# Short products of a two-block transformer kernel laid over all 128 rows of the array, beside zeros

## The chip, the core and the metric

The kernel runs on one core of a Trainium2 chip. A core has a matrix engine (TensorE, in the profile PE, with its weight loads as PEld), VectorE (DVE), ScalarE (ACT), GpSimd (POOL) and SyncE (SP), which here issues the DMAs. Each engine works through its own queue in order; between engines stand semaphores. The metric is the device time of one execution in microseconds (us); the median of the runs counts, and less is better.

## What is computed

Two blocks, one after the other, on 512 tokens of width 1024 in float32. The first block has one layer: a mixer with a state space part (8 heads of 64, two groups with a state of 64) and a stick-breaking attention (8 heads of 64), a cross attention to 256 memory positions, and a feed-forward with squared relu. The second block puts 16 learned tokens ahead (528 positions) and has two layers: gated linear attention over chunks of 64 tokens (4 heads, keys of 128, values of 256), and a sparse attention that scores all keys with 8 small heads of 64, keeps up to 128 of them per query and attends to these; each is followed by a gated feed-forward. The parts that the change is about, from the reference:

```python
logits = jnp.einsum("bhqd,bhkd->bhqk", qb, kb) * scale        # stick-breaking: d = 64
...
S = jnp.exp(tot[:, :, 0, :, None]) * S + jnp.einsum(
    'bhcd,bhce->bhde', ki.astype(jnp.float32) * jnp.exp(tot - cum), vi.astype(jnp.float32))   # c = 64 (first: 16)
...
s_idx = jnp.einsum('bqhd,bsd->bqhs', qib, k_idx) * IDX_DIM ** -0.5    # d = 64
```

In each of them the sum runs over 64 terms, or 16 for the learned tokens.

## The kernel before

All operands of the matrix engine are pairs: a float32 number is split into a high part, in a rounded format that the engine takes at full rate, and a low part, the rest. A product is three matmuls, high by high, high by low and low by high (`mm3`; `mm` is the one place, line 231, where matmuls are issued, and `tr`, line 248, the one for transposes, so nearly all TensorE rows of the profile name one of these two lines). The split is a copy on ScalarE (`hi`, line 272) and a subtraction on VectorE or GpSimd (`lo`, line 275, the engine given by `lo_eng`).

Most of the work are dense products with weight tiles of 128 x 128, in one fixed order (`_tiles`). The weights come in units of 8 tiles by DMA and are split in half units of 4, at most two half units ahead (`w_adv`, three buffers). `dense` runs over the 8 parts of the width, three matmuls each, for 512 token columns, or for 272 and 256 of them in the second block (`FR`). The results lie in PSUM: four banks for dense products (`ps_d`, tag pd) and four for all else (`ps_s`, tag pss).

All else, the side work, is written as generators. `Sched` runs them between the steps of the dense products: each matmul adds its planned time to a clock (`sc.now`), a generator yields how long to wait in this planned time, and `tick` runs those that are due. The build then fixes the order of each engine's queue from a model of the times.

The sites that the change touches:

- `bcast` (418) and `narrow_nat` (521): transposes that bring a norm's column, or a narrow product, from one layout to the other. For the 16 learned tokens and for narrow products they use 16 or 64 rows.
- `mixer` (541): `pair` computes the queries and keys of two heads as one tile of 128 rows, head 0 in rows 0 to 63, head 1 in rows 64 to 127; `ev_q` scales and splits it into two slots of the ring "m" (16 slots). The ring later takes the memory's keys and values and the attention's output. Pairs 0 to 2 are computed beside the state space part, pair 3 behind the values, when `sb_attn` (996) has begun.
- `sb_attn`: for each head and block of 128 queries, `s1` multiplies 64 rows of queries by 64 rows of keys (tile names m,m), then come sigmoids, a running product on VectorE, transposes and the product with the values.
- `ssd` (829): the same with B and C, two groups of 64 rows; `xd` is a tile of its own.
- `gla` (1174): `transp` brings keys and values to a layout by token, 4 blocks of 128, that is two chunks of 64 rows in each (knh, knl, vnh, vnl), and 16 rows for the learned tokens (km, vm). `head` goes through the chunks: products of 64 rows, then the state (`S`, split into Sh and Sl), which the queries' product reads. Then a norm with its own tiles. The gates' narrow product has 48 rows.
- `dsa` (1590): `scores` multiplies queries by the index keys (kih, kil), which lie twice, one above the other, over 128 rows; the second matmul takes only 64 of them. `select` finds the highest scores by 16 rounds of a maximum and a replacement on VectorE. `vproj`, `s2` and `pv` treat the 16 learned tokens as products of 16 rows (vm, pTm).

Of the kernel before, what the change touches and what calls it, by code (L numbers as in the profile page):

```python
# [28 lines left out]
# heads' queries and keys, halves of their values  # L29
# [6 lines left out]
def _tiles():  # L36
# [40 lines left out]
    # second block, first layer  # L77
# [16 lines left out]
    # second layer  # L94
# [66 lines left out]
# a norm's delay behind the last of its squares, the wait before its broadcast (both in us of the tensor  # L161
# engine's work), and whether the dense products queue behind its sums (1), its broadcast (2)
# [15 lines left out]
class Sched:  # L178
    """Runs side work between the steps of the dense products, in the order of the tensor engine's time."""
# [32 lines left out]
class Kern:  # L212
# [95 lines left out]
    def w_adv(self, h):  # L308
        """splits up to half unit h + 2, loads 3 units beyond"""
# [60 lines left out]
    def norm_add(self, n, src, scale=1.0, last=False):  # L370
        """src [128, c0:c1] values by token"""
# [17 lines left out]
    def norm_fin(self, n, dim, eps, wait, urg, bc=True):  # L389
        """generator: n.col[:, i] by token of block i, n.b [128, T2] by token on every partition"""  # L390
# [27 lines left out]
    def bcast(self, out, blocks, col):  # L418
        """out[:, a + j] = col[j, i] for each block (a, m) = blocks[i]"""
# [19 lines left out]
    def after(self, n, fn, cap=2):  # L439
        """fn() once the norm is there; at most cap wait"""  # L440
# [42 lines left out]
    def start2(self):  # L483
        """constants that are needed later"""
# [56 lines left out]
    def mixer(self):  # L541
# [6 lines left out]
        def mslot():  # L548
            return self.til(mix, [P, 512], "m", 16, F32R)
# [54 lines left out]

        def pair(p):
            ((ps, _, _),) = self.dense("w_in", xs, XR)
            q = ev_q(ps, 0.125)
# [16 lines left out]
        # y * silu(z), sums of its squares  # L624
# [37 lines left out]
        # keys and values of the memory  # L662
# [101 lines left out]
    def resid(self, n, rng, norm, xs, g):  # L764
        """the n-th tile of the residual is there: parts of its product with the gain, sums of squares"""
# [63 lines left out]
    def ssd(self, pool, nm, xc, y4, tdt):  # L829
# [4 lines left out]
        BT, CT = [], []  # L834
        for src, dst, nme in ((xc[4], BT, "B"), (xc[5], CT, "C")):
            hi, lo = self.til(pool, [P, 512], nme + "h", 1, F32R), self.til(pool, [P, 512], nme + "l", 1, F32R)
            self.split(hi, lo, src)
            dst += [hi, lo]
# [1136 lines left out]
```

## Time and profile before

| what | value |
|---|---|
| time, median of 3 runs | 2020.23 us (2015.2 to 2020.8) |
| span of the profiled execution | 2017.2 us |
| its time outside the span | not listed apart; the runs lie from 2.0 us below this span to 3.6 above |
| instructions | 29258, of them 11341 matmuls and transposes |
| mean granted clock of TensorE | 0.992 |

How to read the rows that follow: a row of the timeline has start and duration in us, engine, line, operation, the tile written and those read, and the form. The form `64*128 64x256` of a matmul is the weights' rows and columns, then rows and columns of what streams through; the first number, 64, is the rows of the array that the product uses. A row of a tile's view has the count, the shortest, median and longest duration in ns, and the first and last start in us. A row of the windows has, for one stretch of the span, the busy time of each engine with its count of instructions, then the granted clock (PEclk) and the DMAs. A row of the waits has who waited for whom, the sum in us, how often and the longest. A row of the groups has the count, the busy time in us and the mean in ns, and behind a bar the idle time ahead of them. Matmuls are pipelined: a row's duration reaches from its start to the end of its last result, so durations overlap, and the pace is read from start to start.

### The profile page before, as it was taken

What the parts mean: (1) busy time and instruction counts of PE and PEld (TensorE: products, weight loads), DVE (VectorE), ACT (ScalarE), POOL (GpSimd) and SP (SyncE); (2) the same over time, 40 slices, a digit from 0 to 9 for tenths busy, and PEclk for the clock granted to TensorE, in tenths of its full rate; (3) what the DMA queues carried; (4) which work ended last, traced back from release to release, by engine and by line L of the source; (5) the groups of instructions that cost most, each with busy time, mean ns of one, the idle gap of its engine ahead of it and who ended that gap; (6) DMA issues with size and microseconds to landing.
All of it is one profiled execution on the core that took longest, in us unless ns stands there. A gap on an engine that the chain in (4) does not pass through costs nothing.

```text
span 2017.2 us, 29258 instructions
## 1 busy us (share of the span) xinstructions
PE 1986.5 (98%) x11341; PEld 1704.1 (84%) x11341; DVE 1117.3 (55%) x2040; ACT 857.5 (43%) x1636; POOL 358.1 (18%) x323
## 2 busy tenths in 40 slices
PE   8999998999999999999999999999999999999998
PEld 6877777788888888989999999998778888888886
DVE  7788876643344566666444334444898654433444
ACT  6565755542244443445433223333446543323332
POOL 2243342200000211111211001113373021101111
PEclk9999999999999999999999999999999999999999
DMA  5212221422322321212322223323221133233332
GB/s 165 73 64 63 86 71 53 151 94 94 95 94 94 95 75 53 64 43 75 100 85 94 95 84 95 95 86 95 62 74 59 35 96 94 95 94 95 97 96 79
DMA packets 53386, 171.81 MB, mean 85 GB/s; under 512 B 7224, under 2 KB 10808, under 8 KB 53248
## 3 DMA queue, kind: packets, MB, share of 16 engines
q1 hardware_dynamic: 53248, 169.95, 26.9%
q8 instruction: 89, 1.46, 0.3%
q14 instruction: 49, 0.40, 0.1%
HBM read 166.76 MB, written 4.81 MB: 85 GB/s over the span
## 4 chain that ended last, share of the span: by engine, by line
PE 94%; DVE 4%; ACT 1%; issue 1%; POOL 0%; DMA 0%; SPq 0%; DVEq 0%; POOLq 0%
PE pd L231 83%; PE pss L231 9%; PE pss L248 2%; DVE xl L284 1%; DVE swork L1703 1%; DVE m L1702 1%; DVE wlo L275 0%; POOL nacc L387 0%; DVE o L1516 0%; DMA hT<-xT 0%; DVE madd L1707 0%; ACT xh L283 0%; DVE hT L738 0%; ACT whi L272 0%; POOL hT L657 0%
## 5 line engine op out<-in xcount | busy, mean ns | idle before, releaser
L272 ACT ACTIVATE whi<-wraw 128x512 fp32r<-128x512 f32 x600 | 377.0, 630 | 818.2 <-PE pd L231 773.8
L231 PE MATMUL pd<-xh,whi 128*128 128x512 f32 (+2 forms) x2064 | 695.5, 338 | 6.3 <-ACT xh L283 5.5
L231 PE MATMUL pd<-xl,whi 128*128 128x512 f32 (+2 forms) x2064 | 696.2, 338 | 2.2 <-DVE xl L284 2.1
L231 PE MATMUL pd<-xh,wlo 128*128 128x512 f32 (+2 forms) x2064 | 695.8, 338 | 0.4 <-DVE wlo L275 0.3
L275 DVE TENSOR_TENSOR wlo<-wraw,whi 128x512 fp32r<-128x512 f32 x564 | 420.8, 748 | 425.7 <-ACT whi L272 412.0
L231 PEld LDWEIGHTS pd<-xl,whi 128*128 128x128 f32 x2064 | 390.7, 189 | 49.2 <-DVE xl L284 4.3
L231 PEld LDWEIGHTS pd<-xh,whi 128*128 128x128 f32 x2064 | 389.5, 189 | 49.0 <-ACT xh L283 5.9
L231 PEld LDWEIGHTS pd<-xh,wlo 128*128 128x128 f32 x2064 | 390.7, 189 | 45.1 <-DVE wlo L275 1.8
L231 PE MATMUL pd<-hh,whi 128*128 128x512 f32 (+2 forms) x795 | 272.4, 343 | 0.0
L231 PE MATMUL pd<-hl,whi 128*128 128x512 f32 (+2 forms) x795 | 272.0, 342 | 0.0
L231 PE MATMUL pd<-hh,wlo 128*128 128x512 f32 (+2 forms) x795 | 272.0, 342 | 0.0
L387 POOL TENSOR_TENSOR nacc<-nacc,nsq 128x512 f32<-128x512 f32 (+2 forms) x60 | 84.0, 1401 | 561.9 <-ACT nsq L385 556.3
L231 PEld LDWEIGHTS pd<-hh,wlo 128*128 128x128 f32 x795 | 149.4, 188 | 19.3
L231 PEld LDWEIGHTS pd<-hl,whi 128*128 128x128 f32 x795 | 149.4, 188 | 18.8
L231 PEld LDWEIGHTS pd<-hh,whi 128*128 128x128 f32 x795 | 149.4, 188 | 18.6
L1444 POOL TENSOR_TENSOR swg<-swg,nb 128x528 f32<-128x528 f32 (+1 forms) x44 | 57.6, 1308 | 546.5 <-ACT swg L1443 546.5
L1446 DVE TENSOR_TENSOR swg<-pd,swg 128x272 f32<-128x272 f32 (+1 forms) x66 | 32.3, 516 | 64.2 <-PE pd L231 63.6
L1442 DVE TENSOR_TENSOR swg<-pd,nb 128x272 f32<-128x272 f32 (+2 forms) x66 | 32.3, 517 | 64.1 <-PE pd L231 59.7
L275 POOL TENSOR_TENSOR wlo<-wraw,whi 128x512 fp32r<-128x512 f32 x36 | 47.3, 1317 | 61.9 <-ACT whi L272 57.3
L284 DVE SCALAR_TENSOR_TENSOR xl<-hT,cols,xh 128x512 fp32r<-128x512 f32 (+2 forms) x56 | 50.9, 920 | 13.2 <-ACT xh L283 13.0
L283 ACT ACTIVATE xh<-hT,cols 128x512 fp32r<-128x512 f32 (+2 forms) x56 | 36.9, 663 | 26.1 <-DVE hT L1463 9.5
L1086 DVE SCALAR_TENSOR_TENSOR tmp<-pd,nb 128x512 f32<-128x512 f32 x32 | 22.0, 691 | 45.8 <-PE pd L231 44.5
(490 smaller groups left out, 2533.9 us busy)
## 6 DMA issues: line engine op xcount, KB each, us to landing
wraw<-w SPq DMA_DIRECT2D x299, 512.0 KB, 3.5
rrep<-rrow SPq DMA_DIRECT2D x8, 328.0 KB, 6.9
T<-rrep SPq DMA_DIRECT2D x8, 264.0 KB, 2.5
hT<-xT SPq DMA_DIRECT2D x8, 256.0 KB, 5.4
out_dram<-o SPq DMA_DIRECT2D x8, 256.0 KB, 2.2
tmp<-memT SPq DMA_DIRECT2D x8, 128.0 KB, 2.3
wraw<-w SPq DMA_DIRECT2D x2, 256.0 KB, 3.9
qih<-tmp SPq DMA_DIRECT2D x4, 128.0 KB, 2.2
```

Of the source, the lines that this page charges most:

```text
L231: i = self.nc.tensor.matmul(out, lhsT, rhs, start=start, stop=stop)
L248: return self.nc.tensor.transpose(out, in_, self.ident[:n, :n]).ins
L272: self.nc.scalar.activation(out, in_, AF.Copy, scale=scale)
L275: (eng or self.nc.vector).tensor_sub(out, in_, hi.bitcast(F32))
L283: ins = self.nc.scalar.activation(hi, in_, AF.Copy, scale=g)
L284: self.nc.vector.scalar_tensor_tensor(lo, in_, g, hi.bitcast(F32), op0=OP.mult, op1=OP.subtract)
L387: eng.tensor_add(n.acc[:, n.c0 : n.c1], n.acc[:, n.c0 : n.c1], sq[:, n.c0 : n.c1])
L1086: nc.vector.scalar_tensor_tensor(u[:, X], ps, 0.0, nff.b[:, X], op0=OP.max, op1=OP.mult)
L1442: nc.vector.tensor_mul(g[:, c0:c1], p, nf.b[:, c0:c1])
L1444: nc.gpsimd.tensor_mul(g[:, A], g[:, A], nf.b[:, A])
L1446: nc.vector.tensor_mul(g[:, c0:c1], p, g[:, c0:c1])
L1702: nc.vector.max(m8, src)
```

## The change

Every product over 64, 48 or 16 rows gets operands of 128 rows (96 for the 48), of which those that don't belong to it are zero in one of the two.

- Queries of the stick-breaking attention: `ev_heads` makes two pairs of tiles for each pair of heads, each with one head in its half of the rows and zeros, laid by GpSimd, in the other. The keys stay as they are: the other head's rows meet zeros. The ring has 18 slots in place of 16; a pair takes 6 in place of 4.
- State space part: the same with C. To make room, `xd` becomes a temporary tile (`tmp`, three buffers in all).
- Linear attention: the keys by token get 8 blocks, one for each chunk, with zeros in the other half of the rows; two such sets are made once. The first tokens' keys get 128 rows, zeros below the 16, and their values 128 rows of whatever tokens stand there. The tile "ol" has one buffer in place of two, and the norm's two tiles become `q0` and a temporary one. The gates' 48 rows become 96.
- Scores: the second matmul takes all 128 rows; beside the product that it made, this adds the one of the two low parts.
- Sparse attention: the learned tokens' values get zeros below their 16 rows, and their probabilities 128 rows.
- Transposes in `bcast` and `narrow_nat` take 128 rows.

The number of matmuls stays. The rest of the diff takes out comments. Its core:

```diff
@@ bcast @@
-            src = col[:m, i : i + 1].to_broadcast([m, P])
+            src = col[:, i : i + 1].to_broadcast([P, P])
             if m < P:
                 pm = self.ps_s()
-                ins = self.tr(pm[:, :m], src, m)
+                ins = self.tr(pm[:, :P], src)
@@ narrow_nat @@
-        nc.scalar.copy(r[:64, :512], ps[:64, :512])
+        nc.scalar.copy(r[:, :512], ps[:, :512])
...
-            self.tr(pt[:, 64 * i : 64 * i + 64], r[:64, P * i : P * (i + 1)], 64)
-        v = pt[:, :256].rearrange("p (b c) -> p b c", b=4)
+            self.tr(pt[:, P * i : P * (i + 1)], r[:, P * i : P * (i + 1)])
+        v = pt.rearrange("p (b c) -> p b c", b=4)
@@ mixer @@
-            return self.til(mix, [P, 512], "m", 16, F32R)
+            return self.til(mix, [P, 512], "m", 18, F32R)
...
+        def ev_heads(ps, scale):
+            t = self.tmp()
+            nc.vector.scalar_tensor_tensor(t[:, :512], ps, scale, nm.b[:, X], op0=OP.mult, op1=OP.mult)
+            out = []
+            for x in range(2):
+                r, o = slice(64 * x, 64 * x + 64), slice(64 - 64 * x, 128 - 64 * x)
+                hi, lo = mslot(), mslot()
+                nc.gpsimd.memset(hi[o].bitcast(F32), 0.0)
+                nc.gpsimd.memset(lo[o].bitcast(F32), 0.0)
+                self.split(hi[r], lo[r], t[r, :512], self.lo_eng)
+                out.append((hi, lo))
+            return out
         def pair(p):
             ((ps, _, _),) = self.dense("w_in", xs, XR)
-            q = ev_q(ps, 0.125)
+            q = ev_heads(ps, 0.125)
@@ ssd @@
+        BT = [self.til(pool, [P, 512], "B" + x, 1, F32R) for x in "hl"]
+        self.split(BT[0], BT[1], xc[4])
+        CT = []
+        for g in range(2):
+            r, o = slice(64 * g, 64 * g + 64), slice(64 - 64 * g, 128 - 64 * g)
+            CT.append([self.til(pool, [P, 512], f"C{x}{g}", 1, F32R) for x in "hl"])
+            for x in CT[g]:
+                nc.gpsimd.memset(x[o].bitcast(F32), 0.0)
+            self.split(CT[g][0][r], CT[g][1][r], xc[5][r])
...
-            xd = self.til(pool, [P, 512], "xd", 1)
+            xd = self.tmp()[:, :512]
...
-                self.mm3(cb[:, :P], (BT[0][r, C], BT[1][r, C]), (CT[0][r, C], CT[1][r, C]), True, True)
+                self.mm3(cb[:, :P], (BT[0][:, C], BT[1][:, C]), (CT[g][0][:, C], CT[g][1][:, C]), True, True)
...
-                        self.mm3(po[:, cc], (prev[1][r, cc], prev[2][r, cc]), (CT[0][r, C], CT[1][r, C]), True, True)
+                        self.mm3(po[:, cc], (prev[1][:, cc], prev[2][:, cc]), (CT[g][0][:, C], CT[g][1][:, C]), True, True)
@@ sb_attn @@
-            r = slice(64 * hh, 64 * hh + 64)
-            q, k = qk[p]
+            q, k = qk[p][0][hh], qk[p][1]
...
-            self.mm(z[:, :S], q[0][r, t], k[0][r, :S], True, False)
-            self.mm(z[:, :S], q[0][r, t], k[1][r, :S], False, False)
-            self.mm(z[:, :S], q[1][r, t], k[0][r, :S], False, False)
+            self.mm(z[:, :S], q[0][:, t], k[0][:, :S], True, False)
+            self.mm(z[:, :S], q[0][:, t], k[1][:, :S], False, False)
+            self.mm(z[:, :S], q[1][:, t], k[0][:, :S], False, False)
@@ gla @@
-        a2 = gy()[:48, :512]
+        a2 = gy()[:96, :512]
...
-        u = [gy()[:48], gy(F32R)[:48], gy(F32R)[:48]]
+        u = [gy()[:96], gy(F32R)[:96], gy(F32R)[:96]]
...
+        kns = [[self.til(gr, [P, 8, P], f"kn{x}{i}", 1, F32R) for x in "hl"] for i in range(2)]
+        kms = [[self.til(gr, [P, P], f"km{x}{i}", 1, F32R) for x in "hl"] for i in range(2)]
+        for i in range(2):
+            for x in kns[i]:
+                nc.gpsimd.memset(x[0:64, 1::2, :].bitcast(F32), 0.0)
+                nc.gpsimd.memset(x[64:128, 0::2, :].bitcast(F32), 0.0)
+            for x in kms[i]:
+                nc.gpsimd.memset(x.bitcast(F32), 0.0)
...
-            self.tr(pm[:META, :P], t[:, :META])
+            self.tr(pm[:, :P], t[:, :P])
             src = pt.rearrange("p (b e) -> p b e", b=4)
-            self.hi(hi4, src)
-            self.lo(lo4, src, hi4)
-            self.hi(hm, pm[:META, :P])
-            self.lo(lm, pm[:META, :P], hm)
+            for r, hi4, lo4 in parts:
+                self.hi(hi4, src[r])
+                self.lo(lo4, src[r], hi4)
+            m = hm.shape[0]
+            self.hi(hm, pm[:m, :P])
+            self.lo(lm, pm[:m, :P], hm)
...
-                            self.mm3(o, (kn[0][r, b, :], kn[1][r, b, :]), (vn[0][r, b, :], vn[1][r, b, :]), True, True)
+                            self.mm3(o, (kn[0][:, c - 1, :], kn[1][:, c - 1, :]), (vn[0][:, b, :], vn[1][:, b, :]), True, True)
...
-                        t = self.til(gr, [P, 256], "ol", 2)
+                        t = self.til(gr, [P, 256], "ol", 1)
...
-            y = self.til(gr, [P, T2], "gy_", 1)
-            ms = self.til(gr, [P, T2], "gms", 1)
+            y, ms = q0, self.tmp()
...
-                S["vm"] = [self.til(gr, [META, 256], "vm" + x, 2, F32R) for x in "hl"]
+                S["vm"] = [self.til(gr, [P, 256], "vm" + x, 2, F32R) for x in "hl"]
...
-            kn = [self.til(gr, [P, 4, P], "kn" + x, 2, F32R) for x in "hl"]
-            km = [self.til(gr, [META, P], "km" + x, 2, F32R) for x in "hl"]
-            S["t"].append(sc.spawn(transp(t, kn[0], kn[1], km[0], km[1])))
+            kn, km = kns[h % 2], kms[h % 2]
+            parts = [(r, kn[0][r, i::2, :], kn[1][r, i::2, :]) for i, r in enumerate((slice(0, 64), slice(64, P)))]
+            S["t"].append(sc.spawn(transp(t, parts, km[0][:META], km[1][:META])))
@@ run @@
-        wa1 = self.narrow_prep(self.pool(es_gp, "gp", "right"), "w_a1", 16, 48)
+        wa1 = self.narrow_prep(self.pool(es_gp, "gp", "right"), "w_a1", 16, 96)
@@ dsa @@
-                    self.mm(ps, q[r, qs], ki[1][r, c0:c1], False, True)
+                    self.mm(ps, q[:, qs], ki[1][:, c0:c1], False, True)
...
-        vm = [(self.til(pl, [META, 512], "vmh", 2, F32R), self.til(pl, [META, 512], "vml", 2, F32R)) for _ in range(2)]
+        vm = [(self.til(pl, [P, 512], "vmh", 2, F32R), self.til(pl, [P, 512], "vml", 2, F32R)) for _ in range(2)]
+        for a in vm:
+            for x in a:
+                nc.gpsimd.memset(x.bitcast(F32), 0.0)
...
-            self.tr(mt[h][:META, P * b : P * (b + 1)], l[:, :META])
+            self.tr(mt[h][:, P * b : P * (b + 1)], l[:, :P])
             if b == 3:
-                m = mt.pop(h)[:META]
+                m = mt.pop(h)
...
-                self.til(pb, [META, 512], "pTmh", 1, F32R), self.til(pb, [META, 512], "pTml", 1, F32R),
+                self.til(pb, [P, 512], "pTmh", 1, F32R), self.til(pb, [P, 512], "pTml", 1, F32R),
```

More of the change, by code (lines that the diff above doesn't have):

```diff
@@ L833, in ssd @@
         X = slice(META, T2)
[L834 to L838, printed above, removed]
+        BT = [self.til(pool, [P, 512], "B" + x, 1, F32R) for x in "hl"]
[7 more added lines that the diff above has]
+            self.split(CT[g][0][r], CT[g][1][r], xc[5][r])
         for i in range(4):
@@ L915, in ssd @@
             for g in range(2):
-                r = slice(64 * g, 64 * g + 64)
                 cb = self.ps_s()
-                self.mm3(cb[:, :P], (BT[0][r, C], BT[1][r, C]), (CT[0][r, C], CT[1][r, C]), True, True)
+                self.mm3(cb[:, :P], (BT[0][:, C], BT[1][:, C]), (CT[g][0][:, C], CT[g][1][:, C]), True, True)
                 nc.scalar.copy(cbs[:, P * g : P * (g + 1)], cb[:, :P])
@@ L951, in ssd @@
                     po = self.ps_s()
-                    r = slice(64 * g, 64 * g + 64)
                     for i in range(2):
                         cc = slice(P * i, P * i + P)
-                        self.mm3(po[:, cc], (prev[1][r, cc], prev[2][r, cc]), (CT[0][r, C], CT[1][r, C]), True, True)
+                        self.mm3(po[:, cc], (prev[1][:, cc], prev[2][:, cc]), (CT[g][0][:, C], CT[g][1][:, C]), True, True)
                     nc.vector.tensor_mul(E[:, 256 * g : 256 * g + 256], po[:, :256], E[:, 256 * g : 256 * g + 256])
@@ L1187, in gla @@
         nc.sync.dma_start(a2[32:48], self.d["w_a2"])
-        a2h, a2l = gy(F32R)[:48, :512], gy(F32R)[:48, :512]
+        a2h, a2l = gy(F32R)[:96, :512], gy(F32R)[:96, :512]
         self.split(a2h, a2l, a2)
         psa = self.narrow(wa1, xs.tiles, FR, [self.ps_s() for _ in FR])
-        u = [gy()[:48], gy(F32R)[:48], gy(F32R)[:48]]
+        u = [gy()[:96], gy(F32R)[:96], gy(F32R)[:96]]
         def ev_u():
             for ps, c0, c1 in psa:
-                nc.vector.tensor_mul(u[0][:, c0:c1], ps[:48], nb.b[:48, c0:c1])
+                nc.vector.tensor_mul(u[0][:, c0:c1], ps[:96], nb.b[:96, c0:c1])
             self.split(u[1], u[2], u[0])
@@ L1241, in gla, with transp @@
         on = {}
-        def transp(t, hi4, lo4, hm, lm):
+        kns = [[self.til(gr, [P, 8, P], f"kn{x}{i}", 1, F32R) for x in "hl"] for i in range(2)]
[6 more added lines that the diff above has]
+                nc.gpsimd.memset(x.bitcast(F32), 0.0)
+        def transp(t, parts, hm, lm):
             yield 1.2
@@ L1274, in head @@
                         else:
-                            b, r = (c - 1) // 2, slice(64 * ((c - 1) % 2), 64 * ((c - 1) % 2) + 64)
-                            self.mm3(o, (kn[0][r, b, :], kn[1][r, b, :]), (vn[0][r, b, :], vn[1][r, b, :]), True, True)
+                            b = (c - 1) // 2
+                            self.mm3(o, (kn[0][:, c - 1, :], kn[1][:, c - 1, :]), (vn[0][:, b, :], vn[1][:, b, :]), True, True)
                     yield 1.2
@@ L1310, in head @@
                         v = po.rearrange("p (c e a t) -> p c e a t", c=2, e=2, a=2)
-                        t = self.til(gr, [P, 256], "ol", 2)
+                        t = self.til(gr, [P, 256], "ol", 1)
                         tv = t.rearrange("p (e c t) -> p e c t", c=2, e=2)
@@ L1374, in ev_v @@
             S["t"].append(
-                sc.spawn(transp(t, S["vn"][0][:, :, e], S["vn"][1][:, :, e], S["vm"][0][:, e], S["vm"][1][:, e]))
+                sc.spawn(
+                    transp(
+                        t, [(slice(0, P), S["vn"][0][:, :, e], S["vn"][1][:, :, e])], S["vm"][0][:, e], S["vm"][1][:, e]
+                    )
+                )
             )
@@ L1617, in scores @@
             for h in range(8):
-                r = slice(64 * (h % 2), 64 * (h % 2) + 64)
                 q = qi[h // 2][h % 2]
@@ L1747, in vproj @@
             for a, m in [(0, META)] + [(META + P * i, P) for i in range(4)]:
-                p = self.ps_d()[:m]
+                p = self.ps_d()
                 for k in range(2):
-                    ch, cl = cn[k][0][:, a : a + m], cn[k][1][:, a : a + m]
+                    ch, cl = cn[k][0][:, a : a + P], cn[k][1][:, a : a + P]
                     self.mm(p, ch, W[k][0], k == 0, False)
@@ L1753, in vproj @@
                     self.mm(p, cl, W[k][0], False, k == 1)
+                p = p[:m]
                 if m == META:
-                    hi, lo = vm[g]
+                    hi, lo = vm[g][0][:m], vm[g][1][:m]
                 else:
@@ L1765, in vproj @@
                     self.lo(lo, p, hi)
-                out.append((hi, lo))
+                out.append(vm[g] if m == META else (hi, lo))
                 sc.tick()
```

## The prediction

> **What bounds the kernel now.** I read the page first: busy times, then the chain that ended last.
>
> ```profile
> span 2017.2 us, 29258 instructions
> PE 1986.5 (98%) x11341; PEld 1704.1 (84%) x11341; DVE 1117.3 (55%) x2040; ACT 857.5 (43%) x1636; POOL 358.1 (18%) x323
> ...
> PE 94%; DVE 4%; ACT 1%; issue 1%; POOL 0%; DMA 0%; SPq 0%; DVEq 0%; POOLq 0%
> ```
>
> TensorE is busy 98% of the span and is 94% of the chain. A microsecond taken from TensorE is therefore a microsecond of time, unless another engine is close behind at that place. But busy does not say that the array works at its peak: a matmul's row lasts about 0.39 us while the next starts after 0.23 us. What counts is the time from start to start, so I went to the timeline. First the stage of sparse scores, then the linear attention:
>
> ```profile
> 1468.09 0.23 PE L231 MATMUL pss<-kih,qih 128*128 128x144 f32 x1
> 1468.25 0.34 PE L231 MATMUL pss<-kil,qih 64*128 64x144 f32 x1
> 1468.51 0.51 PE L231 MATMUL pd<-xl,whi 128*128 128x512 f32 x1
> 1468.86 0.39 PE L231 MATMUL pd<-xh,wlo 128*128 128x512 f32 x1
> 1469.09 0.40 PE L231 MATMUL pd<-xh,whi 128*128 128x512 f32 x1
> ...
> 794.18 0.28 PE L231 MATMUL pd<-xl,whi 128*128 128x272 f32 x1
> 794.40 0.38 PE L231 MATMUL pss<-vnh,knh 64*128 64x256 f32 x1
> 794.62 0.28 PE L231 MATMUL pss<-vnl,knh 64*128 64x256 f32 x1
> 794.74 0.27 PE L231 MATMUL pss<-vnh,knl 64*128 64x256 f32 x1
> 794.94 0.40 PE L231 MATMUL pd<-xh,wlo 128*128 128x272 f32 x1
> 795.17 0.28 PE L231 MATMUL pd<-xh,whi 128*128 128x256 f32 x1
> 795.29 0.28 PE L231 MATMUL pd<-xl,whi 128*128 128x256 f32 x1
> ```
>
> Three things are to be seen. A full-row matmul starts 0.23 us after one of 512 columns (1468.86 to 1469.09) and 0.12 us after one of 256 (795.17 to 795.29). A 64-row one is no shorter: inside the group 794.62 to 794.74 is 0.12 us as well. But entering and leaving a stretch of 64-row matmuls is dear. From 1468.09 to 1468.86 pass 0.77 us for slots worth at most 0.12 + 0.12 + 0.23 = 0.47: one lone 64-row matmul costs 0.30 us more than its work. From 794.18 to 795.17 pass 0.99 us for five slots worth 0.61: three in a row cost 0.38. So the price is paid **per stretch, not per matmul**, and is about the same for one or three.
>
> The second thing to look at is the granted clock.
>
> ```profile
> core 0: us, PE busy (x) PEld busy (x) DVE busy (x) ACT busy (x) POOL busy (x), PEclk, DMA share, GB/s
> 70.00:141.00 71.00, 71.00 (x371) 57.36 (x370) 56.48 (x84) 44.65 (x103) 30.83 (x22) 1.00 0.21 66
> 141.00:265.00 124.00, 123.09 (x627) 95.90 (x627) 101.28 (x164) 77.31 (x174) 39.03 (x62) 0.99 0.25 77
> 740.00:930.00 190.00, 190.00 (x1305) 169.61 (x1304) 125.11 (x273) 90.87 (x201) 25.80 (x19) 0.96 0.18 56
> 777.90:781.40 3.50, 3.50 (x16) 2.28 (x16) 1.75 (x4) 1.80 (x4) 0.00 (x0) 1.00 0.00 0
> 781.42:784.83 3.41, 3.41 (x18) 3.41 (x17) 1.35 (x4) 0.42 (x1) 0.00 (x0) 0.50 0.44 136
> 1410.00:1480.00 70.00, 70.00 (x328) 51.68 (x327) 59.59 (x125) 30.44 (x67) 28.30 (x24) 1.00 0.21 62
> 1480.00:1525.00 45.00, 39.65 (x172) 31.15 (x171) 42.09 (x105) 24.49 (x47) 33.85 (x26) 0.93 0.23 70
> 1525.00:1660.00 135.00, 134.18 (x750) 111.97 (x749) 90.33 (x261) 75.46 (x174) 23.30 (x18) 1.00 0.21 64
> ```
>
> In the linear attention (740 to 930) the mean clock is 0.96, because of spells of 3.41 us at 0.50, such as the one at 781.42. The 3.5 us before it hold only 16 matmuls of 0.12 us each, about 1.9 us of work, though TensorE counts as busy throughout: the rest is entering and leaving. Four such spells lie in this stage ((1 - 0.96) x 190 = 7.6, against 4 x 1.7 = 6.8 us lost) and one in the first attention (141 to 265).
>
> **The change part by part.** What goes: the stretches of short rows, all but the four 32-row matmuls of the bias rows, which the diff leaves alone. The groups that carry the sum:
>
> ```profile
> L231 PE MATMUL pss<-m,m x96: 270/334/503, 141.4 to 262.9; 64*128 64x128 f32 x24, 64*128 64x256 f32 x24, 64*128 64x384 f32 x24, 64*128 64x512 f32 x24
> ...
> L231 PE MATMUL pss<-vnh,knh x32: 379/382/384, 777.9 to 917.6; 64*128 64x256 f32 x32
> ...
> L231 PE MATMUL pss<-kil,qih x20: 331/386/448, 1408.7 to 1472.4; 64*128 64x272 f32 x8, 64*128 64x400 f32 x4, 64*128 64x256 f32 x4, 64*128 64x144 f32 x4
> L231 PE MATMUL pss<-kil,qil x20: 329/388/449, 1416.2 to 1476.1; 64*128 64x272 f32 x8, 64*128 64x400 f32 x4, 64*128 64x256 f32 x4, 64*128 64x144 f32 x4
> ...
> L231 PE MATMUL pss<-pTmh,vmh x8: 491/496/496, 1534.3 to 1600.8; 16*128 16x512 f32 x8
> ```
>
> Going along the timeline between these first and last starts, I counted stretches and priced each as above, against the slot of a full-row matmul of the same columns. First attention: 96 matmuls in 42 stretches of 0.34 us on the mean, 14.1 us. Linear attention (two more groups of 32 like the one shown, the 16-row products of the first tokens and the 48-row gates): 73 stretches of 0.38, 27.7 us. Scores: 43 of 0.37, 15.9 us. State space part: 15 of 0.22, 3.3 us; where two halves of the rows follow each other there, they overlap, which the change gives up, and the 0.22 is net of it. Sparse attention (two more groups of 8): 13 of 0.33, 4.3 us. Sum 65 us.
>
> Clock: if the five spells come from the thinned work, they go with it: 5 x 1.7 = 8.5 us. Bounds 0 and 8.5; I take 8.5, since the row before the spell shows no other cause.
>
> The Trainium skill, page "TensorE: Matmul & The Clock Gate", Part 1, lays the halved clock to a window in which TensorE idles; by its letter the spells, before which TensorE reads busy, would have another cause and stay, which is rival (e). That rule and the row of 16 matmuls in 3.5 us agree only if thinned work counts as idle.
>
> What is added. The queries of each head pair are split twice over half the partitions, beside zeros; half the partitions cost what all do:
>
> ```profile
> L272 ACT ACTIVATE qih<-tmp x4: 631/632/633, 1397.2 to 1415.2; 64x512 fp32r<-64x512 f32 x4
> ...
> L275 DVE TENSOR_TENSOR knl<-pss,knh x4: 691/692/693, 771.1 to 887.0; 128x512 fp32r<-128x512 f32 x4
> ...
> L1185 POOL MEMSET gy<- x1: 519/519/519, 725.7 to 725.7; 48x512 f32 x1
> ```
>
> So one more ScalarE copy (0.63) and one more VectorE subtraction (0.69) for each of 4 pairs, for C in the state space part and for each of the 4 linear-attention heads: 9 x 0.69 = 6.2 us on VectorE, 5.7 on ScalarE. Some 36 fills of about 0.52 go to GpSimd, 19 us, which lies idle there (busy 30.8 of 71 and 39 of 124); without that cover GpSimd's splits in the state space part would be late by the fills of a pair, 2 us. I take 1.3 us back there, leaving **2.0**.
>
> 141 to 265: VectorE works 101.3 of 124 us. With 0.7 more in 124 - 15.8 = 108 us it is 94% loaded; it is not the bound, but its queue will make weights and transposes late now and then. I take 3 us (bounds 0 and all 14). And there is a new wait. The 18 slots hold three pairs, so pair 3's second head and keys go into pair 0's slots, last read here:
>
> ```profile
> 162.08 0.62 ACT L272 ACTIVATE m<-tmp 128x512 fp32r<-128x512 f32 x1
> ...
> 174.91 0.96 PE L231 MATMUL pss<-m,m 64*128 64x512 f32 x3
> ```
>
> Today the split runs at 162.08; then it can't before about 175. Behind it on ScalarE stand weight splits and the sigmoids that end the wait, so the build must order it late; two of the three temporary tiles stay held for 13 us and the residual's evictions share the third. Bounds 0 and 13; I take 2, nearest to one eviction's delay. Net 14.1 + 1.7 - 5 = **10.8**.
>
> 740 to 930: VectorE 125 of 190 would be 128 of 156. What could be late is the chain of states, below; I take 4 back (bounds 0 and 17). One buffer fewer and results laid into existing tiles cost nothing while heads run one after another. Net 27.7 + 6.8 - 4 = **30.5**.
>
> Scores: VectorE is the bound. It works 59.6 + 42.1 of the 115 us from 1410 to 1525, and TensorE waits there:
>
> ```profile
> PE pd L231 <- DVE khl L275: 4.0, 1, 4.0
> ...
> DVE S L1284 <- PE pss L231: 17.7, 17, 1.6
> ...
> PEld pss L231 <- issue: 9.0, 32, 0.4
> ```
>
> Of 15.9 us only what starts the selection earlier counts: VectorE idles about 10 us before 1480 and hardly after. I take **6** (bounds 0 and 10); the rest becomes a longer wait before the attention's first product. In the attention itself VectorE has slack (90 of 135 us) and the same splits only grow from 16 partitions to 128: **4**. Small rest (norm broadcasts): **0.7**.
>
> Sum 2.0 + 10.8 + 30.5 + 6 + 4 + 0.7 = 54 us. The span would be 1963; the median shown is 3.0 us above this span (runs from 2.0 below it to 3.6 above), so the time is 2020.2 - 54 = **1966**.
>
> **Rivals.** (a) Everything is realised: 65 + 8.5 - 3 = 71 us, **1949**. Against it: VectorE's load in the scores. (b) VectorE and ScalarE bind early: first attention 5, linear attention 18 without the clock, state space 0, scores 3, sparse attention 3, rest 1: 30 us, **1990**. For it: the 94% load. Against: VectorE's idle time is mostly waiting for others. (c) Slower: the chain of states loses its cover.
>
> ```profile
> L275 DVE TENSOR_TENSOR Sl<-S,Sh 128x256 fp32r<-128x256 f32 x36 | 17.3, 489 | 4.7 <-ACT Sh L272 4.5
> L1284 DVE SCALAR_TENSOR_TENSOR S<-S,etot,pss 128x256 f32<-128x256 f32 x32 | 15.3, 478 | 17.9 <-PE pss L231 17.7
> ...
> L272 ACT ACTIVATE Sh<-S 128x256 fp32r<-128x256 f32 x36 | 14.9, 413 | 26.2 <-DVE S L1284 26.1
> ```
>
> Each of 24 steps (4 heads x 6) makes two updates (0.48 us), two copies (0.41) and two subtractions (0.49), 2.8 us, some 3.7 with an estimated 0.15 us for each hand-over, beside 3.0 us of planned dense work (the yields of 1.2 and 1.8) plus, today, the stretches. With the plan's cover alone TensorE waits 0.7 x 24 = 17 us; the sum turns only where over 2.5 us of each step lie bare (24 x 2.5 = 60 us), **2026** or more. Against it: states wait 17.7 us for TensorE, not the other way. (d) The gaps aren't made by rows but by late operands: no gain, **2020**. Against it: the weight loads wait for "issue", nothing that the profile shows. (e) The clock spells stay: 54 - 8.5, **1975**. (f) 64-row products on different halves mostly run at once, and the change gives that up: 48 pairs of the linear attention's 96 products cost 0.12 us more, 5.8 us, in place of the 30.5 won: **2002**. Against it: 0.22 and 0.12 us between the starts at 794.40, 794.62 and 794.74, and today's stretches already count the few pairs that do overlap. The Trainium skill has (f) as a rule on the same page, Part 3: short products in separate row strips run concurrently.
>
> **How the numbers follow.** Forecast 0.52 (alone 1954 to 1978), (a) 0.10, (b) 0.22, (c) 0.04, (d) 0.03, (e) 0.08, (f) 0.01. Faster by over 0.3% (6 us, about what a measurement of this kernel can tell from no change): all but (c) and (d), 0.93; within: 0.03; slower: 0.04. The range takes in the forecast, (e) and most of (b), and stops at the edge of (a): 1950 to 1991.
>
> **What would show it.** Right: no 64-, 48- or 16-row matmuls outside the bias rows; slots of 0.12 and 0.23 throughout 740 to 930; clock 1.00 there; 740 to 930 shorter by about 30 us, 141 to 265 by about 11; VectorE's wait before the sparse attention's first product grown from 4 to about 14 us. Wrong: slots as long with 128 rows (d); idle TensorE in the linear attention waiting for states (c) or for weight splits (b); the half-clock spells still there.

## The result and the profile after

| | before | after |
|---|---|---|
| device time, median (lowest to highest) | 2020.1 us (2015.2 to 2020.8, 4 runs) | 1974.6 us (1973.8 to 1975.4, 4 runs) |
| ratio, with its 95% interval | | 0.9777 (0.9763 to 0.9790) |
| span of the profiled execution | 2017.2 us | 1972.0 us |

The kernel is 45.5 us faster; 54 were forecast. The time lies inside the range, 8.6 us above the predicted 1966. The page of the changed kernel, at the places shown of before:

```profile
span 1972.0 us, 29306 instructions
PE 1924.8 (98%) x11341; PEld 1694.6 (86%) x11341; DVE 1123.1 (57%) x2049; ACT 857.1 (43%) x1643; POOL 372.8 (19%) x359
...
PE 86%; DVE 8%; ACT 2%; issue 2%; POOL 1%; DMA 1%; SPq 0%; DVEq 0%; ACTq 0%; POOLq 0%
```

TensorE's busy time fell by 1986.5 - 1924.8 = 61.7 us, near the 65 us that the stretches were priced at, but the span only by 45.2. The other 16.5 us are new idle time of TensorE. (The clock hardly enters: its mean is 0.992 in both profiles.) The chain says the same: TensorE had 94% of it and has 86%, VectorE's share went from 4% to 8%.

Where each part of the gain arose is read from the first starts of four groups that close a stage, in the groups by tile: first of before, then of after (minimum, median and maximum in ns, then first to last start in us).

```profile
L231 PE MATMUL pss<-m,xqh x32: 276/279/384, 320.6 to 336.6; 128*128 128x256 f32 x32
L231 PE MATMUL pd<-gy,whi x256: 277/283/362, 946.8 to 993.2; 128*128 128x272 f32 x64, 128*128 128x256 f32 x64
L231 PE MATMUL pd<-khh,qah x40: 231/287/535, 1519.0 to 1582.2; 128*128 128x272 f32 x16, 128*128 128x144 f32 x8, 128*128 128x400 f32 x8, 128*128 128x256 f32 x8
L231 PE MATMUL pd<-qah,whi x64: 392/394/504, 1582.8 to 1636.6; 128*128 128x512 f32 x64
```

```profile
L231 PE MATMUL pss<-m,xqh x32: 276/279/384, 318.5 to 334.5; 128*128 128x256 f32 x32
L231 PE MATMUL pd<-gy,whi x256: 277/284/394, 914.6 to 961.3; 128*128 128x272 f32 x64, 128*128 128x256 f32 x64
L231 PE MATMUL pd<-khh,qah x40: 231/287/535, 1478.6 to 1537.8; 128*128 128x272 f32 x16, 128*128 128x144 f32 x8, 128*128 128x400 f32 x8, 128*128 128x256 f32 x8
L231 PE MATMUL pd<-qah,whi x64: 392/394/504, 1538.4 to 1591.4; 128*128 128x512 f32 x64
```

| up to the first start of | before | after | gained in this part | forecast |
|---|---|---|---|---|
| cross attention's scores (pss<-m,xqh): the whole mixer | 320.6 | 318.5 | 2.1 | 2.0 + 10.8 = 12.8 |
| the linear attention's output product (pd<-gy) | 946.8 | 914.6 | 30.1 | 30.5 |
| the sparse attention's first product (pd<-khh) | 1519.0 | 1478.6 | 8.2 | 6 |
| its output product (pd<-qah,whi) | 1582.8 | 1538.4 | 4.0 | 4 |
| the end of the span | 2017.2 | 1972.0 | 0.8 | 0.7 |

Four of the five parts came out within 2.2 us. One did not: the mixer, state space part and first attention together, gave 2.1 us in place of 12.8. The windows of the changed kernel (columns as in the prediction) show where it idles:

```profile
70.00:141.00 71.00, 66.41 (x356) 56.79 (x355) 58.12 (x93) 45.20 (x106) 35.40 (x31) 0.95 0.18 53
101.80:119.00 17.20, 12.61 (x74) 11.15 (x73) 14.38 (x26) 10.62 (x27) 12.84 (x15) 0.80 0.08 29
141.00:265.00 124.00, 117.31 (x658) 100.25 (x656) 107.64 (x169) 79.06 (x181) 41.05 (x66) 0.99 0.29 86
740.00:930.00 190.00, 189.29 (x1557) 187.71 (x1556) 147.55 (x308) 110.04 (x233) 29.05 (x24) 1.00 0.23 70
1410.00:1478.00 68.00, 58.34 (x264) 44.56 (x262) 67.62 (x163) 33.47 (x69) 48.08 (x39) 1.00 0.24 70
```

In the linear attention TensorE is filled, at full clock: there were 0.96 and four half-clock spells. In the scores VectorE works 67.6 of 68 us and TensorE waits for it, as forecast. In the mixer TensorE idles 4.6 us from 101.8 to 119 and 6.7 us from 141 to 265, and for 6.8 us (112.2 to 119.0) its clock is halved. In those 17 us of before TensorE was busy throughout, at full clock. The four largest waits of TensorE in the mixer of the changed kernel, 70 to 285 us (total, times, longest); before, none was over 1.4 us:

```profile
PE pd L231 <- DVE wlo L275: 2.9, 3, 1.6
PE pss L231 <- ACT Mh L272: 2.9, 1, 2.9
PE pss L231 <- ACT wTh L272: 1.6, 1, 1.6
PE pd L231 <- DVE tmp L670: 1.4, 1, 1.4
```

So two questions went to the chip: whether the price of a stretch is right where the gain came as forecast, and what took back 10.7 us in the mixer.

### The profile page after: what moved, and what is told of

Same layout as the page of the kernel before. It is cut to its first block, busy times and chain, and to the rows that moved or that the text cites. A ratio compares the mean times of both kernels' runs of the same rounds, so it can differ in the third digit from the quotient of the medians.

```text
span 1972.0 us, 29306 instructions
## 1 busy us (share of the span) xinstructions
PE 1924.8 (98%) x11341; PEld 1694.6 (86%) x11341; DVE 1123.1 (57%) x2049; ACT 857.1 (43%) x1643; POOL 372.8 (19%) x359
## 4 chain that ended last, share of the span: by engine, by line
PE 86%; DVE 8%; ACT 2%; issue 2%; POOL 1%; DMA 1%; SPq 0%; DVEq 0%; ACTq 0%; POOLq 0%
PE pd L231 78%; PE pss L231 6%; PE pss L248 2%; DVE swork L1733 1%; DVE m L1732 1%; DVE score L1660 1%; DVE wlo L275 1%; DVE xl L284 1%; POOL nacc L387 0%; ACT whi L272 0%; DVE stay L1033 0%; DVE o L1547 0%; DVE y L644 0%; DMA hT<-xT 0%; DVE madd L1737 0%
## 5 line engine op out<-in xcount | busy, mean ns | idle before, releaser
L231 PEld LDWEIGHTS pd<-hh,whi 128*128 128x128 f32 x795 | 149.3, 188 | 18.6
```

The costliest lines, as they stand in the source:

```text
L231: i = self.nc.tensor.matmul(out, lhsT, rhs, start=start, stop=stop)
```

## The experiments

Each kernel's time is the median of its runs, with the lowest and highest; the kernel before, run beside them, had medians of 2017.8 to 2020.7 us.

### Rows alone, in the linear attention

Two kernels put short rows back into the changed kernel and leave everything else. The products of keys and values read the 64 rows that aren't zeros, once all three of a group:

```diff
-                            self.mm3(o, (kn[0][:, c - 1, :], kn[1][:, c - 1, :]), (vn[0][:, b, :], vn[1][:, b, :]), True, True)
+                            r = slice(64 * ((c - 1) % 2), 64 * ((c - 1) % 2) + 64)
+                            self.mm3(o, (kn[0][r, c - 1, :], kn[1][r, c - 1, :]), (vn[0][r, b, :], vn[1][r, b, :]), True, True)
```

> The changed kernel, but the 96 products of keys and values of the linear attention read only the 64 rows that aren't zeros; all else, the zeros and splits too, stays. Changed kernel: 1974.6 us. Theory P (each stretch of short rows costs 0.3 to 0.4 us, and thinned work brings half-clock spells): about 60 stretches, 22 us, and two to four spells of 1.7 us, so 1997 to 2005, linear attention longer by as much. Rival D (the gaps of before came from late operands, not from rows): 1973 to 1977. Rival F (64-row products on different halves run at once): 1969 to 1974.

and once only the second:

```diff
...
+                            self.mm(o, kn[0][:, c - 1, :], vn[0][:, b, :], True, False)
+                            self.mm(o, kn[0][r, c - 1, :], vn[1][r, b, :], False, False)
+                            self.mm(o, kn[1][:, c - 1, :], vn[0][:, b, :], False, True)
```

> The changed kernel, but only the second of the three products of each group of keys and values in the linear attention reads 64 rows (32 products of 96). Changed kernel: 1974.6 us. Theory P (a price of about 0.37 us per stretch, whatever its length): 32 lone stretches, 12 us, 1985 to 1989 with up to two half-clock spells (1.7 us each). Rival M (a price per matmul, 23 us over 96 products, 0.24 us each): 32 x 0.24 = 8 us, 1981 to 1984. Rival D (no price of rows): 1973 to 1977.

Measured: all three 2000.7 us (1996.7 to 2008.4), one 1985.2 us (1984.2 to 1986.7). In the profiles, from the first vnh,knh to the first gy,whi: 139.9 us in the changed kernel (774.7 to 914.6), 151.4 with one short product, 164.5 with three. The groups of the kernel with one:

```profile
L231 PE MATMUL pss<-vnh,knh x32: 274/281/363, 776.1 to 899.0; 128*128 128x256 f32 x32
L231 PE MATMUL pss<-vnl,knh x32: 377/381/387, 776.4 to 899.3; 64*128 64x256 f32 x32
L231 PE MATMUL pd<-gy,whi x256: 277/284/392, 927.5 to 974.1; 128*128 128x272 f32 x64, 128*128 128x256 f32 x64
```

11.5 us over 32 lone products is 0.36 us each, the price that the prediction put on a stretch (0.38). One of them in its timeline:

```profile
793.31 0.28 PE L231 MATMUL pd<-xh,wlo 128*128 128x256 f32 x1
793.42 0.28 PE L231 MATMUL pss<-vnh,knh 128*128 128x256 f32 x1
793.54 0.28 PE L231 MATMUL pd<-xh,whi 128*128 128x272 f32 x1
793.75 0.38 PE L231 MATMUL pss<-vnl,knh 64*128 64x256 f32 x1
794.06 0.39 PE L231 MATMUL pd<-xl,whi 128*128 128x272 f32 x1
794.29 0.28 PE L231 MATMUL pss<-vnh,knl 128*128 128x256 f32 x1
```

The full-row vnh,knh stands between dense products at 0.11 and 0.12 us. The 64-row vnl,knh, on the same operands' tiles and of the same 256 columns, stretches three slots: 0.21 before it, 0.31 its own, 0.23 behind it, 0.75 us in place of some 0.37. That the gaps came from late operands (rival D) is refuted. With three short products of three, the timeline has the 96 of them in 61 stretches, 46 of them lone; they cost 24.6 us, 3.4 of it in two half-clock spells. The rest is 21.2 / 61 = 0.35 us per stretch, as in the other kernel; per matmul it would be 0.22 here and 0.36 there. So a price per matmul (M) is refuted too. The Trainium skill, page "TensorEngine Tiling (Array Packing)", section Key Properties, says that a change of the tiling mode drains TensorE; it gives no price, and these rows agree with it if going from 128 rows to 64 is such a change.

Not every number of rows below 128 is paid for. The gates' products went from 48 rows to 96, not to 128, and 96 cost nothing. In the changed kernel:

```profile
740.02 0.29 PE L231 MATMUL pd<-xl,whi 128*128 128x272 f32 x1
740.15 0.53 PE L231 MATMUL pss<-gy,gy 96*128 96x272 f32 x3
740.52 0.29 PE L231 MATMUL pd<-xh,wlo 128*128 128x272 f32 x1
```

The slot ahead of the three is 0.13 us and the three take 0.37, as dense products would. With 48 rows, in the kernel before, the same two stretches were 0.21 and 0.56 us (740.84, 741.05 and 741.61). The prediction's price is one of 64, 48 or 16 rows; between 64 and 96 nothing was tried.

The spells came with the short rows, behind windows that the profile shows as busy. The first of the two in the kernel with three:

```profile
793.00:796.40 3.40, 3.40 (x14) 2.14 (x14) 0.94 (x3) 0.53 (x2) 0.00 (x0) 1.00 0.00 0
796.40:799.80 3.40, 3.40 (x18) 3.40 (x17) 1.67 (x4) 1.42 (x3) 0.00 (x0) 0.51 0.00 0
```

14 matmuls in 3.4 us, then 3.4 us at half the clock, as in the kernel before. One short product of three brought no spell: the linear attention's clock stayed at 1.00.

### Which term of the mixer fell

Three kernels undo one part each, a fourth takes load from VectorE. The first attention's 96 score products at 64 rows, the splits and fills kept:

```diff
-            self.mm(z[:, :S], q[0][:, t], k[0][:, :S], True, False)
+            r = slice(64 * hh, 64 * hh + 64)
+            self.mm(z[:, :S], q[0][r, t], k[0][r, :S], True, False)
...
```

> The changed kernel, but the 96 score products of the first attention read only the 64 rows that aren't zeros; the double splits, the fills and the ring of 18 stay. Changed kernel: 1974.6 us. Theory B (the first attention isn't bound by TensorE any more: VectorE and the order of its queue set when weights, transposes and values are ready, so that the time of the rows is only exchanged for idle time): 1974 to 1980. Rival T (TensorE's rows set it, as the prediction had it, and something else in the mixer was lost at the same time): 42 stretches of 0.34 us come back, 1986 to 1990.

The whole first attention as before, xd and E in tiles of their own:

```diff
-            return self.til(mix, [P, 512], "m", 18, F32R)
+            return self.til(mix, [P, 512], "m", 16, F32R)
...
-            q = ev_heads(ps, 0.125)
+            q = ev_q(ps, 0.125)
...
-            xd = self.tmp()[:, :512]
+            xd = self.til(pool, [P, 512], "xd", 1)
...
```

> The changed kernel with the first attention as it was before (queries split once, 64 rows, no fills, 16 slots), and xd and E in tiles of their own; the state space part keeps its 128 rows. Changed kernel: 1974.6 us. Theory B (first attention bound by VectorE and its order): 1971 to 1979, since 6 us of splits go from VectorE as the rows come back. Rival T (rows set it): 10 to 14 us slower, 1985 to 1989, less what the ring costs.

The state space part as before, xd and E in tiles of their own (C in one pair of tiles, its products and those of prev on 64 rows):

> The changed kernel with the state space part as it was before: C is split once, its products use 64 rows, xd and E have tiles of their own; the first attention keeps its 128 rows. Changed kernel: 1974.6 us. Theory H (the hand-over from the state space part to the attention, the 5.6 us of waits at 103 to 113 with the shared ring or the 6.2 us at 148 with the shared slot of E, costs what the rows bring): 1964 to 1969. Theory B (VectorE binds the first attention wherever the hand-over lies): 1972 to 1977. The forecast price of the rows of this part is 3.3 us.

Work taken from VectorE:

```diff
-            (nc.gpsimd if j == 2 else nc.vector).tensor_mul(be[:, :S], be[:, :S], st[:, 1 : S + 1])
+            (nc.vector if j == 0 else nc.gpsimd).tensor_mul(be[:, :S], be[:, :S], st[:, 1 : S + 1])
```

> The changed kernel, but 16 of the products of beta and stay in the first attention (256 and 512 columns, 11 us on VectorE) go to GpSimd, which idles there 83 of 124 us. Changed kernel: 1974.6 us. Theory B with VectorE's load as its cause: VectorE at 97 instead of 108 of 124 us, fewer of the 7.7 us of waits, 1967 to 1972. Theory B with the order of queues or the chain of one unit as its cause: 1973 to 1978, or slower, since the product takes longer on GpSimd (0.9 us against 0.7).

| kernel | median, us | against the changed kernel's 1974.6 | ratio to before (the changed kernel's: 0.9777, 0.9763 to 0.9790) |
|---|---|---|---|
| sb_three | 1986.9 (1982.9 to 1989.2) | +12.3 | 0.9842 (0.9819 to 0.9865) |
| sb_undone | 1983.9 (1980.9 to 1986.1) | +9.3 | 0.9828 (0.9806 to 0.9850) |
| ssd_undone | 1977.0 (1974.9 to 1977.9) | +2.4 | 0.9795 (0.9774 to 0.9816) |
| relief | 1972.7 (1971.8 to 1973.4) | -1.9 | 0.9773 (0.9753 to 0.9794) |

The changed kernel's 1974.6 was not measured beside these four. By the ratios to the kernel before, the first two are slower than it; ssd_undone and relief can't be told from it.

My first theory was that VectorE's load had eaten the gain (B). It fell: the rows of the first attention are worth 12.3 us in the changed kernel, near the 10.8 that the prediction gave them, and relief brings nothing that is clear of noise. (Relief is also a weaker test than planned: 11 us less work for VectorE were expected, and its busy time fell by 7.9, from 1123.1 to 1115.2.) In the profile of sb_three the mixer is 13.0 us longer than the changed kernel's, with 4.7 us less idle time of TensorE and 3.4 us more lost at half clock; that leaves 14.3 us for the rows, and the prediction had counted 14.1. Rival T stood: the rows pay, and something else in the mixer costs as much. (sb_undone came 1 us below T's range.) ssd_undone was to settle whether that was the hand-over from the state space part; it missed its range for H by 8 us, since it has the wait that it was to be rid of, 6.3 us for the attention's values. It told only that this wait comes neither from the rows of the state space part nor from a slot that xd and E share.

### The tile that moved

One line of the diff takes xd from the ring of three temporary tiles. Two kernels isolate it. The kernel before with that line alone:

```diff
-            xd = self.til(pool, [P, 512], "xd", 1)
+            xd = self.tmp()[:, :512]
```

> The kernel before with one line of the change: xd is taken from the ring of three temporary tiles. No row count and no split is changed. Kernel before: 2020.1 us. Theory R (the shared ring holds the evictions back): slower by 6 to 12 us, 2026 to 2032, with a stretch without dense products between about 100 and 120 us. Theories V (splits and fills) and S (slots of the ring m): 2019 to 2021.

and the changed kernel without it; there is no room for a further tile, so xd takes E's slot, which is free while xd lives:

```diff
-            xd = self.tmp()[:, :512]
+            xd = self.til(pool, [P, 512], "xd", 1)
...
-                E = self.til(pool, [P, 512], "E", 1)
+                E = self.til(pool, [P, 512], "xd", 1)
```

> The changed kernel, but the scaled inputs xd of the state space part no longer share the ring of three temporary tiles with the evictions of queries and keys; they share the slot of E instead. Changed kernel: 1974.6 us. Theory R (the shared ring holds the evictions of pairs 0 to 2 back until the last xd is written, from about 79 to 115.8 us, so that dense products run out of banks at 101.8): the first eviction of a query is back at about 80 us, dense products stand among the state space products again, and the time falls by 8 to 12 us, to 1963 to 1967. Theory V (the additional splits and fills load VectorE, ScalarE and GpSimd): 1973 to 1976. Theory S (the 18 slots of the ring m hold pair 3 back): 1973 to 1976.

The line alone makes the kernel before slower by 14.0 us: 2034.7 (2033.8 to 2035.3) against 2020.7, ratio 1.0073 (1.0059 to 1.0087); 6 to 12 were expected. Part of it is clock: of the 16.1 us between the two profiled spans, 8.5 are half-clock spells. In its timeline the first eviction of a query moves from 79.4 to 114.8 us, right behind the fourth xd (114.2). VectorE's timeline of the changed kernel shows the same:

```profile
115.15 0.69 DVE L919 TENSOR_TENSOR tmp<-pss,dt 128x512 f32<-128x512 f32 x1 [1.98 <-PE pss L248]
115.76 0.68 DVE L608 SCALAR_TENSOR_TENSOR tmp<-pd,nb 128x512 f32<-128x512 f32 x1
```

The first line is the last of four writes of xd; the second is the first eviction of a query. The program runs the state space part ahead of the first pair, so in the ring all four xd are drawn before pair 0's queries. In VectorE's queue their evictions stand behind the fourth xd, which waits for its transposes until 115.15 us. With xd in E's slot the same eviction stands here:

```profile
80.35 0.69 DVE L608 SCALAR_TENSOR_TENSOR tmp<-pd,nb 128x512 f32<-128x512 f32 x1
```

35 us earlier. In between the four banks of the dense products fill up with pairs 0 and 1, and from 101.8 to 118.7 us TensorE has only the state space chain, one step at a time, with the wait of 2.9 us for Mh. After that wait the clock is halved:

```profile
108.80:112.20 3.40, 1.15 (x5) 0.53 (x4) 3.13 (x8) 3.06 (x10) 1.55 (x2) 1.00 0.02 5
112.20:119.00 6.80, 6.03 (x27) 5.74 (x28) 4.75 (x11) 3.98 (x8) 5.84 (x9) 0.50 0.00 0
```

Yet xd in E's slot gives 1975.6 us (1974.3 to 1976.7), no gain where R expected 8 to 12 us. The early evictions came back, and the time did not: counted in the timelines, its 450th dense product starts 17 us earlier than the changed kernel's, and its 700th 1.5 us later. A new wait stands in between, 5.8 us for the attention's values at 148 us.

### The hand-over behind it

The chain of waits of the kernel with xd in E's slot, in order of time (start, length, what), from the last state space results to the values:

```profile
143.85 0.44 DVE y L1009
...
144.31 0.70 DVE y L644
...
145.10 0.63 ACT nacc L382
...
145.73 1.28 ACT L642
...
147.03 0.64 ACT tmp L642
...
147.74 1.29 POOL tmp L643
...
149.05 1.74 DVE y L644
```

After it come the attention's first scans (DVE stay, beta) and then the eviction vl, at 153.37. The fourth of z's gates needs the fourth temporary tile of a ring of three, which is free only when the first result y has been multiplied; by then ScalarE has to load another table for it (the row of 1.28 us, ACT_TABLE_LOAD in the timeline). The chain isn't new. In the kernel before the values were evicted at almost the same time:

```profile
152.00 0.75 DVE L646 SCALAR_TENSOR_TENSOR vl<-pd,ncol,vh 128x512 fp32r<-128x512 f32 x1
...
152.80 0.50 PE L231 MATMUL pd<-xh,whi 128*128 128x512 f32 x1 [0.31 <-DVE vl L646]
```

There TensorE, slower by its short rows, came to the wait at 152.5 and lost 0.31 us. Now it comes at 148.4. To try that, in the kernel with xd in E's slot the gates are multiplied in place, so that the fourth temporary tile no longer waits for a result y:

```diff
...
             nc.scalar.activation(t[:, :512], zt[i], AF.Sigmoid)
-            nc.gpsimd.tensor_mul(t[:, :512], t[:, :512], zt[i])
-            nc.vector.tensor_mul(y4[:, i, :], y4[:, i, :], t[:, :512])
+            nc.gpsimd.tensor_mul(zt[i], zt[i], t[:, :512])
+        for i in range(4):
+            nc.vector.tensor_mul(y4[:, i, :], y4[:, i, :], zt[i])
...
```

> The kernel with xd in E's slot (1975.6 us), and besides the four gates are multiplied in place as soon as z is there, so that the fourth gate doesn't wait for a temporary tile that only the state space result frees. Theory H (the wait of 5.8 us for the values of the first attention at 148 us comes from the chain of last state space product, result, fourth gate, result, on whose end the values' evictions queue): the wait shrinks to 2 to 4 us and the time falls to 1971 to 1974. Rival C (the chain of the units of the first attention sets its end): the wait shrinks, and later waits grow by as much, 1974 to 1977.

The same with less work for VectorE, and the same with the state space part at 64 rows; beside them the changed kernel again:

> The kernel gate_early with the 16 products of beta and stay on GpSimd instead of VectorE. If the waits of the first attention after 200 us come from VectorE's load, 3 to 5 us below gate_early; if they come from the chain of its units, within 2 us of it.

> The kernel ssd_undone (64 rows in the state space part, 1977.0 us) with the four gates in place as in gate_early. Theory H: its wait for values of 6.3 us shrinks by 2 to 4 us, 1972 to 1975; if the rows of the state space part (3.3 us forecast) are worth anything here, it is slower than gate_early by up to that. Rival C: 1976 to 1979.

> The changed kernel as it is, beside the next three on the same chip: 1974.6 us, 1972 to 1977 if its time is the same on another chip.

| kernel | median, us | ratio to before |
|---|---|---|
| after_again | 1974.4 (1973.7 to 1975.4) | 0.9777 (0.9762 to 0.9793) |
| gate_early | 1968.1 (1965.6 to 1968.9) | 0.9744 (0.9727 to 0.9760) |
| gate_relief | 1969.6 (1968.4 to 1970.4) | 0.9752 (0.9736 to 0.9769) |
| gate_ssd_undone | 1972.3 (1971.1 to 1975.4) | 0.9768 (0.9751 to 0.9785) |

gate_early beats both kernels: 6.3 us below the changed one, their runs apart. The mixer's end in its profile:

```profile
L231 PE MATMUL pss<-m,xqh x32: 276/279/384, 309.8 to 325.8; 128*128 128x256 f32 x32
```

320.6 - 309.8 = 10.8 us are gained in the mixer, of the 12.8 forecast. It gained more than H had said (7.5 us below xd_own, not 2 to 5), and not in the way that H had said. The wait at 148 shrank as expected: TensorE waits there 3.4 us, by the profile for GpSimd's sums of squares. But the values come no earlier: their first eviction (vl) starts at 153.05 us, in xd_own at 153.37. What changed is what stands in the wait. TensorE goes on with the norm's sums and products of the attention before the values come, where xd_own idled until they came. By the end of the mixer this kernel is 9.2 us ahead of xd_own, with 5.3 us less idle time and 3.4 us less lost at half clock.

gate_relief is no faster: what is left doesn't look like VectorE's load (its busy time fell by only 3.7 us here). gate_ssd_undone is 4.2 us slower than gate_early; at the same mean clock, 0.991, their runs are 1971.5 and 1968.8 to 1968.9 us, 2.6 apart. As the splits and fills go with these rows, this stands beside the net 2.0 us forecast, and it is little more than the spread of the runs. The gates in place with xd still in the ring were not tried, so how much of the gain each of the two steps would bring alone isn't known.

## Why the prediction was right, and where it wasn't

- **The price per stretch** was right: 0.36 us for a lone product, measured, against 0.38. TensorE's busy time fell by 61.7 of 65 us.
- **Linear attention, 30.5 us**: 30.1. Its clock went to 1.00 as forecast; the spells went with the short rows and two came back with them. The chain of states took next to nothing in place of the 4 us: TensorE idles 0.7 of 190 us, which refutes (c). That the sum fits so closely is in part luck. In this part of the span the half clock takes 1.7 us (a spell at 730.0) in place of 6.8, so 5.1 came back and not 6.8; idle time grew by 0.7; that leaves 25.7 us for the rows, not 27.7, and the errors cancel. Rivals (d) and (f) are refuted by the kernels with rows put back; (e) too for this stage. The estimate of 0.15 us for a hand-over in (c) was high: in the trace of before a copy starts 0.03 to 0.10 us after its update where nothing else holds it.
- **Scores, 6 us**: 8.2. The bound was VectorE, as forecast. Where it would show was wrong: the wait before the attention's first product stayed at 4.0 us (pd for khl). TensorE's other waits grew, spread over the scores (waits from 1380 to 1495 us of the changed kernel; the last two were not there before):

```profile
PE pd L231 <- DVE khl L275: 4.0, 1, 4.0
PE pd L231 <- POOL wlo L275: 2.3, 3, 1.1
PE pss L231 <- ACT srel L1655: 1.8, 3, 1.4
```

- **Sparse attention, 4 us, and the rest, 0.7**: 4.0 and 0.8.
- **First attention, 10.8 us**: its rows are worth 12.3 in the changed kernel. The size was right; the gain was taken elsewhere in the mixer. TensorE's idle time up to the cross attention went from 12.0 to 23.0 us, and half clock took 6.8 us in place of 3.4. With these 14.4 us the 2.1 gained become 16.5, and the rows of both parts had been priced at 14.1 + 3.3 = 17.4. In gate_early idle time is 18.6 us and half clock 3.4, so the rows gave 10.8 + 6.6 = 17.4.
- **State space part, 3.3 less 1.3 taken back**: this is the step that failed. It priced rows, splits and fills, and left out that the edit moves xd into the ring of temporary tiles. That results laid into existing tiles cost nothing was said of the linear attention, where heads run one after another, and nothing there speaks against it; in the state space part such a move costs 14.0 us in the kernel before. In the changed kernel this cost doesn't show alone: without it the wait for the values takes its place (xd_own), and with the gates in place besides, the gain comes back. The prediction knew that the evictions draw on that ring (it counted its three tiles where pair 3 waits) and didn't ask in which order the tiles are drawn.
- **The hand-over to the values**: the prediction didn't ask what would be late next there. The values' eviction started at 152.0 us in the kernel before and at 153.4 in xd_own, and TensorE was going to be there 4 us earlier.
- **Pair 3's wait for slots** did come as described, in gate_early, as ScalarE's timeline shows: 2.60 us for the scores that read the old tile. What it cost in time isn't known; 2 us had been taken.
- **Rival (b)**, VectorE and ScalarE as the bound in the mixer, would have given a similar time for another reason. The two kernels with less work for VectorE (-1.9 and +1.5 us) speak against it.
- **The clock, 8.5 us, and rival (e)**: the total of 1974.6 us is the number of (e), 54 - 8.5 = 45.5 us and 1975, and that is chance. (e) had the spells stay, and the four of the linear attention went. But others came: the spells of the two traces sum to 34.3 us before and 30.3 after, at half clock, so the clock gave 2.0 us over the whole span and not 8.5. The 8.6 us between forecast and time are nearly the mixer's 10.7, less the 2.2 that the scores gave beyond theirs.

## What to carry to other kernels

Count what it costs to enter and leave a stretch of products with fewer rows, not the products: zeros in the unused rows bought 0.36 us each time here, and half-clock spells besides. Filling 48 rows up to 96 was enough. When an edit makes room by moving a tile into a shared ring, list all users of the ring in the order of the program: a tile drawn early by a slow chain holds back everyone behind it, however idle the engines are. And when TensorE gets faster ahead of a chain on other engines, look up at what time that chain ends today: that is where the gain stops, unless work from behind it can be put into the wait.

## What the hardware showed that was not expected

The half-clock spells of the linear attention went, but the kernel's mean clock stayed at 0.992: others came in the mixer, at 112.2 (6.8 us), 146.3 and 265.8 us, where the kernel before had two (252.4 and 310.4). In the 3.4 us ahead of the three, TensorE worked 1.15, 1.68 and 1.73 us. The Trainium skill, page "TensorE: Matmul & The Clock Gate", Part 1, ties the halved clock to a window of about 3.4 us in which TensorE idles; these three spells agree with it only if a window that is idle for half or two thirds is enough. The one at 796.4 us of gla_three doesn't go by the busy time: its window reads 3.40 of 3.40 us busy, with 14 matmuls. Nor does the new one at 730.0 of the changed kernel, where 18 of the 31 matmuls ahead of it have a single column. If the wait for Mh brought the spell at 112.2, which no run isolates, it cost twice its length: 2.9 us, and up to 3.4 us for the 6.8 us at half the clock behind it.
